# Counting one of six token tiles on ScalarE in a threshold search

## The chip, the cores and the metric

The kernel runs on one core of a Trainium2 chip. A core has a matrix engine (TensorE, PE in the profile), three engines for elementwise work (VectorE, DVE; ScalarE, ACT; GpSimd, POOL), an engine that here only issues transfers (SyncE, SP), and 16 DMA engines. Each engine has a queue of its own and works through it in the order in which the program put it there; engines wait for each other by semaphores. The metric is the time of one execution on the device in microseconds (us), the median of several runs.

## The reference

One layer of a streaming encoder for 1024 tokens of width 1024. After a modulated norm, one combined projection of 4816 columns gives the inputs of two attention branches and the merge gates. In the sparse branch each token picks the 256 keys with the highest index score, out of the keys of its own chunk of 64 and of all earlier chunks:

```
dots = jnp.einsum('bqhd,bkd->bqhk', qi[:, start:end], ki[:, :end])
score = jnp.einsum('bqh,bqhk->bqk', wi[:, start:end], jax.nn.relu(dots))
score = jnp.where(allowed[None], score, -jnp.inf)
_, idx = lax.top_k(score, kk)
```

Softmax and the weighted sum of the values then run over the picked keys. After both branches come the gated merge, the output projection, a second norm, and a mixture of 32 experts with two experts per token.

## The kernel before, in words

**Tokens.** The 1024 tokens are 8 tiles of 128. Tile i has (i+1)*128 keys. Tiles 0 and 1 need no search (at most 256 keys). Tiles 2 to 7 each have a table `score[i]` of 128 x (i+1)*128 floats in on-chip memory, and `masks[i]`, which holds a bf16 copy of the upper half of each score until the search ends and the finished mask from then on.

**The search.** `select(tiles)` finds each row's 256th highest score by setting the bits of a threshold one after the other, from bit 30 down to bit 0. For a bit, VectorE compares each tile of the group with its threshold and adds up the hits (L722, one pass over the tile; bits 30 to 16 read the bf16 copy, bits 15 to 0 the floats), then two operations on 128x3 numbers (L725, L727) settle the bit and set the next one. So one bit's passes must end before the next bit's begin. Two searches run interleaved, one for tiles 2, 3, 4 and one for tiles 5, 6, 7; the text calls one bit of both a round. After bit 0, seven operations per tile (L733 to L740) make the mask, with ties in order of index.

**What sets the order.** The program text is written by generators that a class `Feed` interleaves. The projection loops call `feed.unit(650)` after each unit, which is three 128x128 by 128x512 products (a three-term product of split floats, L166 to L168). Each unit gives the search a budget of 650 times `feed.share` ns, and the search puts operations into the queues until the sum of its own cost estimates has used it up: 0.52 ns per key and 70 per pass for bits above 15, 1.04 ns per key and 70 otherwise, 100 for each small operation. These estimates decide where in each queue a search operation stands, and nothing else.

**Stages around the search.** With u for the units counted from the first one of the index projection: columns FQ at u 112 to 175 (share 0.3), three chunks of gate columns at u 176 to 367 (share 1.05), FV at u 368 to 431, FK from u 432. Before FK the rest of the search is put into the queues (`feed.drain_search`). A gate chunk takes 64 units: 8 products of 128 tokens-by-columns tiles, in the groups of 16, 8, 8, 8, 8, 16 units (`gate_chunk`). Each product gathers in one of three PSUM buffers `mm`, taken in turn, and ScalarE empties it with a sigmoid (L826), then issues the store to `gate_d`. The 8 slices of the next chunk's weights are converted one by one: ScalarE makes `wh` (L160), GpSimd `wl` (L163). In FK, ScalarE copies and squares each product (L860, L756), VectorE sums and normalises it, and TensorE transposes the result (L641) in between its products.

Of the kernel before, what the change touches and what calls it, by code (L numbers as in the profile page):

```python
# [19 lines left out]
F32 = mybir.dt.float32  # L20
F32R = mybir.dt.float32r
BF = mybir.dt.bfloat16
# [3 lines left out]
AF = mybir.ActivationFunctionType  # L26
OP = mybir.AluOpType
# [3 lines left out]
P = 128  # L31
T = 1024
D = 1024
NT = T // P
# [36 lines left out]
def kernel(ctx, tc, x, c, positions, ada_w, ada_b, norm1_g, norm2_g, w_in, b_fgt, b_gate,  # L71
# [3 lines left out]
    V, A, G, PE = nc.vector, nc.scalar, nc.gpsimd, nc.tensor  # L75
# [12 lines left out]
    def dump(name, ap):  # L88
        if name in dbg:
            SY.dma_start(dbg[name], ap)  # L90
# [64 lines left out]
    def bc(ap, shape):  # L155
        return ap.to_broadcast(shape)
# [327 lines left out]
    masks = {b: kvp2.tile([P, (b + 1) * P], BF, name=f"mask{b}") for b in range(2, NT)}  # L484
# [33 lines left out]
    def wtile(name):  # L518
        bufs = 1 if name == "t1" else 2
        feed.take(name, bufs)  # L520
        return wk.tile([P, H, HD], F32, name=name, bufs=bufs)

    def rope(dst, src, n, i=None, eng=G):

        if i is None:
            c4 = bc(cos[:, :, None, :], [P, n, 2, 32])
            s3 = bc(sin, [P, n, 32])
        else:
            c4 = bc(cos[:, i, None, None, :], [P, n, 2, 32])
            s3 = bc(sin[:, i, None, :], [P, n, 32])  # L530
        s4 = src.rearrange("p n (a d) -> p n a d", a=2)
        d4 = dst.rearrange("p n (a d) -> p n a d", a=2)
        t4 = wtile("t1").rearrange("p n (a d) -> p n a d", a=2)
        eng.tensor_tensor(t4[:, :, 0], s4[:, :, 1], s3, op=OP.mult)
        eng.tensor_tensor(t4[:, :, 1], s4[:, :, 0], s3, op=OP.mult)
        V.tensor_tensor(d4, s4, c4, op=OP.mult)
        yield 2
        V.tensor_tensor(d4[:, :, 0], d4[:, :, 0], t4[:, :, 0], op=OP.subtract)
        V.tensor_tensor(d4[:, :, 1], d4[:, :, 1], t4[:, :, 1], op=OP.add)
        feed.give("t1")  # L540
# [83 lines left out]
    xs = sX.enter_context(tc.tile_pool(name="xs", bufs=1, side="right"))  # L624
    score = {b: xs.tile([P, (b + 1) * P], F32, name=f"score{b}") for b in range(2, NT)}
    jk = xs.tile([P, T], BF, name="jk")
# [3 lines left out]
    def turned_heads(src, stack, dst, eng=G):  # L630

        st = stack()
        A.activation(st[:, :, 0].bitcast(F32R), src, AF.Copy)
        yield 1
        eng.tensor_tensor(st[:, :, 1].bitcast(F32R), src, st[:, :, 0], op=OP.subtract)
        yield 6
        feed.give("qr")
        for g in range(2):
            tp = ptb.tile([P, 4, P], F32, name="tpB")
            for j in range(4):  # L640
                PE.transpose(tp[:, j, :], st[:, g * 4 + j], ident)  # L641
            if g == 1:
                feed.give("stack")
            yield 1
            A.activation(dst(g), tp, AF.Copy)

    KSEL, scored = 256, []

    def index_scores(i, ps):
        q = wtile("q")
        A.activation(q, ps, AF.Copy)  # L653
        yield 1
        qr = wtile("qr")
        yield from rope(qr, q, H, i)
        feed.give("q")
        yield 1
        feed.take("stack", 2)
        feed.take("qT", 2)  # L660
        qT = xsa.tile([P, H, P], F32, name="qT", bufs=2).bitcast(F32R)
        yield from turned_heads(qr, lambda: xsa.tile([P, H, 2, HD], F32, name="stackx", bufs=2),
                                lambda g: qT[:, g * 4:g * 4 + 4])
        yield 1
        n = (i + 1) * P
        last = None

        def weigh(h, c0, w, pd):
            rl = xs.tile([P, 512], F32, name="rl", bufs=3)
            A.activation(rl[:, :w], pd[:, :w], AF.Relu)  # L670
            sc = score[i][:, c0:c0 + w]
            wc = wix[:, i, h:h + 1]
            if h == 0:
                V.tensor_scalar(sc, rl[:, :w], wc, None, op0=OP.mult)
            else:
                V.scalar_tensor_tensor(sc, rl[:, :w], wc, sc, op0=OP.mult, op1=OP.add)

        for h in range(H):
            for c0 in range(0, n, 512):
                w = min(512, n - c0)  # L680
                pd = psx.tile([P, 512], F32, name="pd")
                PE.matmul(pd[:, :w], qT[:, h], ikh[:, c0:c0 + w], start=True, stop=False)
                PE.matmul(pd[:, :w], qT[:, h], ikl[:, c0:c0 + w], start=False, stop=True)
                if last:
                    weigh(*last)
                last = (h, c0, w, pd)
                yield 1 if c0 else 0
        weigh(*last)
        feed.give("qT")
        dump(f"score{i}", score[i])  # L690
        V.memset(score[i][0:CH, n - CH:n], LOW)

        yield 2
        A.activation(masks[i], score[i].bitcast(BF).rearrange("p (n two) -> p n two", two=2)[:, :, 1], AF.Copy)
        yield 1
        scored.append(i)
        for grp in ((2, 3, 4), (5, 6, 7)):
            if i in grp and set(grp) <= set(scored):
                feed.search.append(select(grp))

    def select(tiles):


        m = len(tiles)
        bits = xs.tile([P, m], U32, name="bits", bufs=2)
        drop = xs.tile([P, m], U32, name="drop", bufs=2)
        cnt = xs.tile([P, m], F32, name="cnt_", bufs=2)
        thr = bits.bitcast(F32)

        for g, i in enumerate(tiles):  # L710
            n = (i + 1) * P
            V.tensor_scalar(jk[:, :n], score[i], 0.0, 0.0, op0=OP.is_ge, op1=OP.add, accum_out=cnt[:, g:g + 1])
            yield n * 1.04 + 70
        V.tensor_scalar(drop, cnt, KSEL - 0.5, float(2 ** 31), op0=OP.is_lt, op1=OP.mult)
        V.tensor_scalar(bits.bitcast(I32), drop.bitcast(I32), 31, 1 << 30, op0=OP.arith_shift_right,
                        op1=OP.bitwise_xor)


        for b in range(30, -1, -1):
            for g, i in enumerate(tiles):  # L720
                n = (i + 1) * P
                V.tensor_scalar(jk[:, :n], masks[i] if b > 15 else score[i], thr[:, g:g + 1], 0.0, op0=OP.is_ge,  # L722
                                op1=OP.add, accum_out=cnt[:, g:g + 1])
                yield n * (0.52 if b > 15 else 1.04) + 70
            V.tensor_scalar(drop, cnt, KSEL - 0.5, float(2 ** b), op0=OP.is_lt, op1=OP.mult)  # L725
            yield 100
            V.scalar_tensor_tensor(bits, bits, (1 << b) >> 1, drop, op0=OP.bitwise_xor, op1=OP.bitwise_xor)  # L727
            yield 100
        for g, i in enumerate(tiles):
            n = (i + 1) * P  # L730
            s = score[i]
            th, need = thr[:, g:g + 1], cnt[:, g:g + 1]
            V.tensor_scalar(jk[:, :n], s, th, 0.0, op0=OP.is_gt, op1=OP.add, accum_out=need)  # L733
            V.tensor_scalar(need, need, -1.0, float(KSEL), op0=OP.mult, op1=OP.add)
            V.tensor_scalar(jk[:, :n], s, th, None, op0=OP.is_equal)
            cs = xs.tile([P, 512], F32, name="rl", bufs=3).bitcast(F16)
            V.tensor_tensor_scan(cs[:, :n], bc(ones[:, 0:1], [P, n]), jk[:, :n], 0.0, op0=OP.mult, op1=OP.add)
            V.scalar_tensor_tensor(jk[:, :n], cs[:, :n], need, jk[:, :n], op0=OP.is_le, op1=OP.mult)
            V.scalar_tensor_tensor(jk[:, :n], s, th, jk[:, :n], op0=OP.is_gt, op1=OP.add)
            V.tensor_scalar(masks[i], jk[:, :n], -1.0, -NEG, op0=OP.add, op1=OP.mult)  # L740
            yield n * 5.98 + 600
# [6 lines left out]

    feed.rate = 4
    tokens(C_IQ, spread(index_scores), (4, 7, 6, 5, 3, 2))  # L750
    feed.rate, feed.share = 2, 0.05

# [40 lines left out]
    for i in range(2):  # L793
        masks[i] = kvp3.tile([P, (i + 1) * P], BF, name=f"mask{i}")
        n = (i + 1) * P
# [560 lines left out]
    for s_ in range(NT + 1):  # L1356
# [6 lines left out]
        if s_ < NT:  # L1363
            g = dsa_scores(s_)
# [141 lines left out]
    key = rtp2.tile([P, P], F32, name="key")  # L1506
# [16 lines left out]
    cnt = rtp2.tile([P, NE], F32, name="cnt")  # L1523
# [652 lines left out]
```

## Time and profile before

| | us |
|---|---|
| median of 3 runs (1690.26 to 1699.87) | 1691.45 |
| the profiled execution | 1688.29 |
| its span (first to last instruction) | 1686.5 |
| PE busy | 1535.2 (91%) |
| VectorE busy | 1001.4 (59%) |
| ScalarE busy | 562.9 (33%) |
| GpSimd busy | 343.3 (20%) |

The page cuts the span into 40 slices of 42.2 us. A digit is the busy share of an engine in tenths; PEclk is the clock that TensorE was granted, in tenths of full speed. The search lies in slices 4 to 10 (about 195 to 455 us).

### The profile page before, as it was taken

What the parts mean: (1) busy time and instruction counts of PE and PEld (TensorE: products, weight loads), DVE (VectorE), ACT (ScalarE), POOL (GpSimd) and SP (SyncE); (2) the same over time, 40 slices, a digit from 0 to 9 for tenths busy, and PEclk for the clock granted to TensorE, in tenths of its full rate; (3) what the DMA queues carried; (4) which work ended last, traced back from release to release, by engine and by line L of the source; (5) the groups of instructions that cost most, each with busy time, mean ns of one, the idle gap of its engine ahead of it and who ended that gap; (6) DMA issues with size and microseconds to landing.
All of it is one profiled execution on the core that took longest, in us unless ns stands there. A gap on an engine that the chain in (4) does not pass through costs nothing. (4 is left out here: it accounts for less than half of the span.)

```text
span 1686.5 us, 29265 instructions
## 1 busy us (share of the span) xinstructions
PE 1535.2 (91%) x10694; PEld 1020.3 (60%) x10695; DVE 1001.4 (59%) x2562; ACT 562.9 (33%) x1278; POOL 343.3 (20%) x376
## 2 busy tenths in 40 slices
PE   5999999999299999999998999699999899989993
PEld 4877878888287677765555777444444444544441
DVE  6688889999941877667664866422433434244331
ACT  5576242222163776546543433111111111111110
POOL 3333422222041432211003400001111111111110
PEclk9999999999699999999999999899999999999997
DMA  9300333331003331454555764889999999999992
GB/s 295 117 26 26 106 106 92 98 100 51 0 13 123 84 83 26 132 195 149 160 163 159 198 230 176 332 316 340 380 372 354 372 364 366 354 360 362 364 343 74
DMA packets 162282, 335.65 MB, mean 199 GB/s; under 512 B 31927, under 2 KB 78039, under 8 KB 162128
## 3 DMA queue, kind: packets, MB, share of 16 engines
q1 hardware_dynamic: 136368, 295.25, 50.7%
q0 software_dynamic: 11776, 20.93, 5.8%
q10 hardware_dynamic: 13984, 17.50, 2.9%
q8 instruction: 87, 1.43, 0.4%
q14 instruction: 67, 0.55, 0.1%
HBM read 299.02 MB, written 36.75 MB: 199 GB/s over the span
## 5 line engine op out<-in xcount | busy, mean ns | idle before, releaser
L1934 PE MATMUL pab<-block,gx 128*32 128x256 f32 (+1 forms) x2752 | 242.1, 428 | 4.5 <-DMA block<-in_exp_w 3.3
L2000 DVE SCALAR_TENSOR_TENSOR ys<-py,inf,gt 32x256 f32<-32x256 f32 (+2 forms) x178 | 97.6, 548 | 136.3 <-PE py L1980 52.5
L1934 PEld LDWEIGHTS pab<-block,gx 128*32 128x32 f32 (+1 forms) x2752 | 105.5, 117 | 113.6 <-issue 53.4
L1914 ACT ACTIVATE gx<-tpe,aff 128x64 f32<-128x64 f32 (+2 forms) x124 | 42.4, 422 | 327.5 <-PE tpe L1905 327.5
L163 POOL TENSOR_TENSOR wl<-wraw,wh 128x512 fp32r<-128x512 f32 x68 | 91.3, 1353 | 192.6 <-ACT wh L160 189.4
L1800 DVE COPY inf<-tpe 128x2 f32<-128x2 f32 x32 | 5.1, 159 | 207.6 <-PE tpe L1780 207.6
L166 PE MATMUL mm<-wh,hh 128*128 128x512 f32 x304 | 122.6, 403 | 0.5 <-ACT q L653 0.4
L168 PE MATMUL mm<-wh,hl 128*128 128x512 f32 x304 | 119.5, 393 | 0.0
L167 PE MATMUL mm<-wl,hh 128*128 128x512 f32 x304 | 119.5, 393 | 0.0
L166 PE MATMUL mm<-hh,wh 128*128 128x512 f32 x256 | 100.5, 393 | 0.0
L168 PE MATMUL mm<-hh,wl 128*128 128x512 f32 x256 | 99.7, 389 | 0.0
L167 PE MATMUL mm<-hl,wh 128*128 128x512 f32 x256 | 99.6, 389 | 0.0
L1795 POOL DMA_INDIRECT hg<-h_d,ix x31 | 31.1, 1003 | 309.7 <-issue 224.0
L722 DVE TENSOR_SCALAR_CACHE_REDUCE jk<-score,bits 128x768 bf16<-128x768 f32 (+2 forms) x96 | 90.7, 944 | 1.7
L1987 POOL DMA_INDIRECT out<-ys,ix x32 | 47.1, 1472 | 214.5 <-DVE ys L2000 201.9
L1926 PE MATMUL pab<-block,gx 128*128 128x512 f32 x192 | 85.9, 600 | 0.5
L722 DVE TENSOR_SCALAR_CACHE_REDUCE jk<-mask,bits 128x768 bf16<-128x768 bf16 (+2 forms) x90 | 85.0, 944 | 1.6
L1960 ACT ACTIVATE tx<-tpe 128x256 f32<-128x256 f32 (+2 forms) x32 | 14.9, 464 | 160.2 <-PE tpe L1958 160.2
L1001 DVE CUSTOM_DVE_ANT_0 zt<-psf,fb 128x1024 f32<-128x1024 f32 (+7 forms) x64 | 48.1, 754 | 31.4 <-PE psf L1071 22.7
L168 PEld LDWEIGHTS mm<-wh,hl 128*128 128x128 f32 x304 | 57.7, 190 | 12.6
L166 PEld LDWEIGHTS mm<-wh,hh 128*128 128x128 f32 x304 | 57.8, 190 | 11.6 <-ACT q L653 0.8
L1980 PE MATMUL py<-block,tx 128*32 128x256 f32 x1152 | 64.8, 380 | 0.0
(447 smaller groups left out, 3413.9 us busy)
## 6 DMA issues: line engine op xcount, KB each, us to landing
block<-in_exp_w SPq DMA_DIRECT2D x384, 512.0 KB
wraw<-in_w_in SPq DMA_DIRECT2D x72, 256.0 KB
adw<-in_ada_w SPq DMA_DIRECT2D x16, 1024.0 KB
xt<-in_x SPq DMA_DIRECT2D x16, 512.0 KB
gt<-gate_d SPq DMA_DIRECT2D x32, 256.0 KB
gate_d<-q ACTq DMA_DIRECT2D x30, 256.0 KB
adaw<-in_ada_w SPq DMA_DIRECT2D x4, 1024.0 KB
xt<-in_ada_w SPq DMA_DIRECT2D x8, 512.0 KB
```

What stands on the lines that cost most here:

```text
L163: eb.tensor_tensor(lo, src, hi.bitcast(F32), op=OP.subtract)
L166: PE.matmul(ps, lh, rh, start=first, stop=False)
L167: PE.matmul(ps, lh, rl, start=False, stop=False)
L168: PE.matmul(ps, ll, rh, start=False, stop=last)
L722: V.tensor_scalar(jk[:, :n], masks[i] if b > 15 else score[i], thr[:, g:g + 1], 0.0, op0=OP.is_ge, op1=OP.add, accum_out=cnt[:, g:g + 1])
L1001: V.tensor_tensor_reduce(zt[:, :n], ps[:, :n], add, -0.125, -LOW, op0=OP.add, op1=OP.min, accum_out=st[:, 0:1])
L1914: A.activation(gx[:, k, :n], tp[:, k, :n], AF.Identity, scale=scale, bias=shift)
L1926: PE.matmul(ps[:, m * 512:(m + 1) * 512], gx[:, k], r[:, m, kk * 512:(kk + 1) * 512], start=k == 0, stop=last)
L1934: PE.matmul(ps[c * n:(c + 1) * n, g * 8 * n:(g + 1) * 8 * n].rearrange("p (m f) -> p m f", m=2), gx[:, k, g * n:(g + 1) * n], w[:, c], sta ...
L1980: PE.matmul(py[c * 32:(c + 1) * 32, g * 256:(g + 1) * 256], tx[:, g, q * 32:(q + 1) * 32], r[:, m, c * 256:(c + 1) * 256], start=q == 0 an ...
L1987: G.indirect_dma_start(out=out, out_offset=bass.IndirectOffsetOnAxis(ap=ix, axis=0), in_=ys, in_offset=None, compute_op=OP.add, bounds_che ...
L2000: V.scalar_tensor_tensor(ys[r, f], py[c * n:(c + 1) * n, g * w:(g + 1) * w], inf[r, 6:7], gt2[r, f], op0=OP.mult, op1=OP.mult)
```

## The change

Tile 7, the longest, is counted on ScalarE. For it the search puts into ScalarE's queue one pass `Sign(threshold - score)` over 128x1024 with a running sum (new L728) and one 128x1 operation that turns the sum into the count that the settling step expects (new L730); VectorE's pass for that tile goes. The ScalarE pass adds 0 to the cost estimate (`yield 0`). It always reads the floats, so the bf16 copy of tile 7 (L694) is no longer made; its elementwise output goes to `masks[7]` as a place to write. Tile 7 comes first in its group. Since a sum of signs treats a score equal to the threshold otherwise than a comparison does, tile 7 gets six more VectorE operations after bit 0 (one pass over 1024 keys, five on 128x1).

```diff
-    KSEL, scored = 256, []
+    KSEL, ON_A, scored = 256, NT - 1, []
...
-        A.activation(masks[i], score[i].bitcast(BF).rearrange("p (n two) -> p n two", two=2)[:, :, 1], AF.Copy)
+        if i != ON_A:
+            A.activation(masks[i], score[i].bitcast(BF).rearrange("p (n two) -> p n two", two=2)[:, :, 1], AF.Copy)
...
+        tiles = sorted(tiles, key=lambda i: i != ON_A)
...
+        sums = xs.tile([P, 2], F32, name="sums", bufs=2) if ON_A in tiles else None
...
         for b in range(30, -1, -1):
             for g, i in enumerate(tiles):
                 n = (i + 1) * P
+                if i == ON_A:
+                    A.activation(masks[i], score[i], AF.Sign, scale=-1.0, bias=thr[:, g:g + 1],
+                                 accum_out=sums[:, 0:1])
+                    A.activation(cnt[:, g:g + 1], sums[:, 0:1], AF.Copy, scale=-0.5, bias=0.5 * n + 0.25)
+                    yield 0
+                    continue
                 V.tensor_scalar(jk[:, :n], masks[i] if b > 15 else score[i], thr[:, g:g + 1], 0.0, op0=OP.is_ge,
                                 op1=OP.add, accum_out=cnt[:, g:g + 1])
...
+            if i == ON_A:
+                ulp = sums[:, 1:2]
+                V.scalar_tensor_tensor(ulp, th, -1.0, th, op0=OP.mult, op1=OP.max)
+                V.scalar_tensor_tensor(th, ulp, 2.0 ** -126, th, op0=OP.is_ge, op1=OP.mult)
+                V.tensor_scalar(jk[:, :n], s, th, 0.0, op0=OP.is_gt, op1=OP.add, accum_out=need)
+                V.tensor_scalar(ulp, ulp, 1.2 * 2.0 ** -24, None, op0=OP.mult)
+                V.scalar_tensor_tensor(ulp, need, KSEL - 0.5, ulp, op0=OP.is_ge, op1=OP.mult)
+                V.tensor_tensor(th, th, ulp, op=OP.add)
```

**VectorE, one late round.** Before (`score5` to `score7` are tiles 5 to 7, `cnt__1662` the counts of that group, `jk` a scratch output):

```order
L722 TENSOR_SCALAR jk_856,cnt__1662<-score5_853,bits_1660 128x768
L727 SCALAR_TENSOR_TENSOR bits_2108<-bits_2108,drop_2109 128x3
L722 TENSOR_SCALAR jk_856,cnt__1662<-score6_854,bits_1660 128x896
L722 TENSOR_SCALAR jk_856,cnt__2110<-score2_850,bits_2108 128x384
L722 TENSOR_SCALAR jk_856,cnt__1662<-score7_855,bits_1660 128x1024
L722 TENSOR_SCALAR jk_856,cnt__2110<-score3_851,bits_2108 128x512
L725 TENSOR_SCALAR drop_1661<-cnt__1662 128x3
L722 TENSOR_SCALAR jk_856,cnt__2110<-score4_852,bits_2108 128x640
```

Now:

```order
L733 TENSOR_SCALAR jk_856,cnt__1661<-score5_853,bits_1659 128x768
L733 TENSOR_SCALAR jk_856,cnt__2113<-score2_850,bits_2111 128x384
L733 TENSOR_SCALAR jk_856,cnt__1661<-score6_854,bits_1659 128x896
L733 TENSOR_SCALAR jk_856,cnt__2113<-score3_851,bits_2111 128x512
L736 TENSOR_SCALAR drop_1660<-cnt__1661 128x3
L733 TENSOR_SCALAR jk_856,cnt__2113<-score4_852,bits_2111 128x640
L738 SCALAR_TENSOR_TENSOR bits_1659<-bits_1659,drop_1660 128x3
```

The 1024-wide pass is gone; four passes stand between the setting of the bits and the step L736 that needs ScalarE's count.

**ScalarE, the end of the second gate chunk and the start of the third.** Before (`wh` is a converted weight slice, `mm` a PSUM buffer, `q` the sigmoid's output):

```order
L160 ACTIVATE wh_3285<-wraw_2977 128x512
L160 ACTIVATE wh_3298<-wraw_3224 128x512
L826 ACTIVATE q_3308<-mm_3201,bgc_70 128x512
L827 DMA gate_d_79<-q_3308 128x512
L826 ACTIVATE q_3311<-mm_3202,bgc_70 128x512
L827 DMA gate_d_79<-q_3311 128x512
L160 ACTIVATE wh_3321<-wraw_3238 128x512
L160 ACTIVATE wh_3337<-wraw_3253 128x512
L826 ACTIVATE q_3399<-mm_3314,bgc_70 128x512
```

Now:

```order
L728 ACTIVATE mask7_801,sums_1662<-score7_855,bits_1659 128x1024
L730 ACTIVATE cnt__1661<-sums_1662 128x1
L160 ACTIVATE wh_3364<-wraw_3026 128x512
L160 ACTIVATE wh_3378<-wraw_3297 128x512
L846 ACTIVATE q_3388<-mm_3275,bgc_70 128x512
L847 DMA gate_d_79<-q_3388 128x512
L846 ACTIVATE q_3391<-mm_3276,bgc_70 128x512
L847 DMA gate_d_79<-q_3391 128x512
L160 ACTIVATE wh_3401<-wraw_3315 128x512
L728 ACTIVATE mask7_801,sums_1662<-score7_855,bits_1659 128x1024
L730 ACTIVATE cnt__1661<-sums_1662 128x1
L160 ACTIVATE wh_3419<-wraw_3329 128x512
```

The last two of the 31 passes L728 (bits 1 and 0) stand ahead of, and between, the sigmoids and conversions of the second chunk's end. All 31 stand in ScalarE's queue ahead of the third chunk's first sigmoid: 4 in FQ, 27 from the first gate unit on. The last search operation of VectorE stood in the middle of FV before and now stands in the third gate chunk. No table load of ScalarE is added, and no transfer of SP's queue changes place.

## Rows read from the trace of the kernel before

**Rows 1.** The page, part 2: busy tenths and granted clock in 40 slices.
```profile
PE   5999999999299999999998999699999899989993
DVE  6688889999941877667664866422433434244331
PEclk9999999999699999999999999899999999999997
```
**Rows 2.** Stretches: us, PE, PEld, DVE, ACT, POOL busy (x), PEclk, DMA share, GB/s.
```profile
238.70:412.80 174.10, 174.10 (x769) 144.01 (x769) 168.29 (x435) 45.59 (x72) 41.82 (x36) 1.00 0.29 88
432.60:462.30 29.70, 0.01 (x2) 0.04 (x1) 26.79 (x48) 3.55 (x9) 1.88 (x2) 0.56 0.00 0
462.30:495.00 32.70, 32.70 (x157) 27.13 (x158) 15.43 (x34) 17.28 (x39) 10.34 (x9) 0.93 0.04 11
```
**Rows 3.** Waits, longest first: us in total, times, longest.
```profile
PE tpB L641 <- DVE stack L635: 29.7, 1, 29.7
```
**Rows 4.** Timeline of DVE: start, duration; the first gate-phase round to the mask's end.
```profile
244.55 1.14 DVE L722 TENSOR_SCALAR_CACHE_REDUCE jk<-mask,bits 128x896 bf16<-128x896 bf16 x1
246.39 1.28 DVE L722 TENSOR_SCALAR_CACHE_REDUCE jk<-mask,bits 128x1024 bf16<-128x1024 bf16 x1
...
398.04 1.28 DVE L722 TENSOR_SCALAR_CACHE_REDUCE jk<-score,bits 128x1024 bf16<-128x1024 f32 x1
...
399.37 0.75 DVE L722 TENSOR_SCALAR_CACHE_REDUCE jk<-score,bits 128x512 bf16<-128x512 f32 x1
...
404.06 1.28 DVE L722 TENSOR_SCALAR_CACHE_REDUCE jk<-score,bits 128x1024 bf16<-128x1024 f32 x1
...
416.76 1.28 DVE L722 TENSOR_SCALAR_CACHE_REDUCE jk<-score,bits 128x1024 bf16<-128x1024 f32 x1
...
419.88 1.01 DVE L733 TENSOR_SCALAR_CACHE_REDUCE jk<-score,bits 128x768 bf16<-128x768 f32 x1
...
454.69 0.33 DVE L740 TENSOR_SCALAR mask<-jk 128x640 bf16<-128x640 bf16 x1
```
**Rows 5.** Timeline of ACT: end of FQ, end of FV, and the queue around the 30 us.
```profile
238.72 0.60 ACT L777 ACTIVATE q<-mm 128x512 f32<-128x512 f32 x1 [1.41 <-PE mm L168]
...
412.92 1.28 ACT L844 ACTIVATE vf<-mm 128x512 f32<-128x512 f32 x2 [1.36 <-PE mm L168]
...
424.77 0.61 ACT L860 ACTIVATE q<-mm 128x512 f32<-128x512 f32 x1
455.65 0.60 ACT L756 ACTIVATE sq<-mm 128x512 f32<-128x512 f32 x1 [30.27 <-DVE sm L758]
```
**Rows 6.** Groups by line, ACT: count | busy us, mean ns | idle before.
```profile
L160 ACT ACTIVATE wh<-wraw 128x512 fp32r<-128x512 f32 x72 | 44.3, 631 | 28.7 <-PE mm L167 12.4 <-PE mm L168 10.6 <-DMA wraw<-in_w_in 3.9
L826 ACT ACTIVATE q<-mm,bgc 128x512 f32<-128x512 f32 x30 | 20.7, 689 | 94.9 <-PE mm L168 89.0 <-ACT q L826 2.8 <-DMA gate_d<-q 2.6
L1004 ACT ACTIVATION_READ_ACCUMULATOR zt<-zt,smf 128x1 f32 x64 | 12.4, 194 | 0.0
L401 ACT ACTIVATE hh<-xT,mod 128x1024 fp32r<-128x1024 f32 x8 | 9.5, 1235 | 3.6 <-DVE mod L397 3.6
L1004 ACT ACTIVATE zt<-zt,smf 128x1024 f32<-128x1024 f32 x8 | 9.1, 1143 | 0.2
L294 ACT ACTIVATE jx<-xt 128x1024 bf16<-128x1024 f32 x8 | 8.4, 1050 | 2.4 <-DMA xt<-in_x 2.4
L172 ACT ACTIVATE smo<-smo 128x1 f32<-128x1 f32 x8 | 1.6, 196 | 1.9 <-DVE smo L171 1.9
```
**Rows 7.** Short stretches around the wait, columns as in group 2.
```profile
432.00:437.00 5.00, 0.60 (x3) 0.18 (x1) 4.75 (x10) 0.00 (x0) 0.00 (x0) 0.94 0.00 0
437.00:442.00 5.00, 0.00 (x0) 0.00 (x0) 4.86 (x7) 0.00 (x0) 0.00 (x0) 0.50 0.00 0
466.00:467.00 1.00, 1.00 (x3) 0.73 (x3) 0.00 (x0) 0.15 (x1) 0.00 (x0) 0.50 0.00 0
467.00:468.00 1.00, 1.00 (x6) 0.80 (x5) 0.00 (x0) 0.00 (x0) 0.00 (x0) 0.95 0.00 0
```

## The prediction

> **What bounds the kernel now.** I read the page's slices first, to find the stage that the search touches. TensorE is at nine tenths nearly throughout, except one slice at 2, the eleventh (422 to 464 us), and there its granted clock is the lowest, too. VectorE is at nine tenths in the five slices up to it [rows 1]. So the search sets the time in one place. The list of waits names it: one wait of 29.7 us, TensorE for `stack`, which VectorE writes in FK [rows 3]. The table of stretches shows the same from both sides: from 238.7 to 412.8 TensorE never pauses (769 products, 256 units, 0.680 us each) while VectorE is 97% busy; from 432.6 to 462.3 TensorE does nothing [rows 2]. The timeline of VectorE tells what it does meanwhile: bit 0's last passes, and from 419.9 to 455.0 the masks [rows 4]; only then come FK's sums.
>
> Two readings matter more than that wait. **The queue lags behind its text.** A clear round takes 404.06 - 398.04 = 6.02 us [rows 4], but the planner books a round above bit 15 at 3.0 us (4224 keys x 0.52, six passes x 70, four small steps x 100) and a lower one at 5.2. So VectorE's search operations stand in the text well ahead of when VectorE gets to them. Before, that hurts nobody, since TensorE and ScalarE wait for no search result until FK. **What a waiting ScalarE holds up.** ScalarE's square for FK waited 30.27 us for VectorE, with all of FK's later evictions behind it [rows 5].
>
> **The change, part by part.**
>
> *Removed from VectorE:* 31 passes of 1024 keys. One takes the slot 398.04 to 399.37, 1.33 us [rows 4], so a clear round falls from 6.02 to 4.69. It is no cheaper on the bf16 copy: the pass at 246.39 also took 1.28 [rows 4].
>
> *Added to ScalarE:* 31 times Sign with a sum. The trace has no Sign, so I bound it by 1024-wide rows: 1.05 us (a square to bf16) and 1.24 (identity to split floats); nearest is Exp with a sum, 1.14, and its accumulator read 0.19; the 128x1 step after it 0.20 [rows 6]. With gaps 1.6 us. VectorE asks for the count after four passes (of 768, 384, 896, 512 keys, some 3.6 us of the 4.69), so ScalarE has 2 us to spare at either bound and the round stays 4.69. In sum 50 us on an engine that is busy for 45.6 of the 174.1 us [rows 2]: room enough. The bf16 copy that goes and the operations after bit 0 that come (one pass, 1.3 us, and five tiny ones, together about 2) cost nothing: the masks now end near 412 and FK starts some 45 us later; without that cover it would be 2 us.
>
> *Moved, and here is the cost:* each Sign waits for a bit that VectorE has to set, and behind it in ScalarE's queue stand sigmoids that free PSUM buffers, and conversions of the next weights. With three buffers TensorE can run one or two products ahead of a sigmoid, no more. So the lag of VectorE, until now free, becomes TensorE's pace. Even the cheaper rounds are slower than booked (2.4 us above bit 15, 4.1 below), so VectorE stays behind to the end.
>
> **The sum.** First VectorE. The order has four rounds ahead of the gates, where the trace had three; so 27 rounds are left, and I let them start where the first gate-phase round did, at 244.6 [rows 4]. Before, 27 rounds took 416.76 - 246.39 = 170.4 us, 8 more than 27 x 6.02; in that time GpSimd converted four chunks' slices, and I charge the 8 us to its work. Two chunks' conversions fall into the new rounds: 4 us. Rounds end at 244.6 + 27 x 4.69 + 4 = 375.2, bit 1's Sign starts two rounds earlier, at 365.8.
>
> Then TensorE. The third chunk's first pair of products needs two buffers. The second of them is freed by a sigmoid that stands behind bit 1's Sign and two conversions: 365.8 + 1.6 + 2 x 0.63 + 0.69 [rows 6] = 369.4. From there 127 units lie ahead of FK, without any Sign in the way that matters: 127 x 0.680 = 86.4, FK starts at 455.8. Is TensorE really waiting then? Its last long stop before is for a sigmoid behind bit 11's Sign: 244.6 + 15 x 4.69 + 2 + 1.6 + 0.69 = 319.2; from there 63 units take it to 362. So it waits some 7 us again. Without any stop TensorE would have been at this unit at 238.7 + 129 x 0.680 = 326.4, so the stops add up to 43 us; by the places of the sigmoids there are five, of 5 to 11 us each.
>
> The clock: after the end of products at 432.6 the granted clock averaged 0.94 up to 437 and was 0.50 after, and after the restart at 462.3 it stayed at 0.50 (1.2 GHz) until about 467 [rows 7]: 4.7 us at half speed, 2.4 us lost. In the long wait it was down in the second 5 us, so I take it to be down after a stop of 7 us as well and charge 2.4 us for the last one. For the earlier ones I charge nothing, because TensorE waits for ScalarE again after each.
>
> Before, FK started at 412.8 and then lost 29.7 and 2.4 us, as if it had started at 444.9. Now: 455.8 + 2.4 = 458.2, with no wait in FK. So **+13.3 us**. Behind FK every stage waits for the one ahead (the expert weights, too, are loaded into space that the attention gives back), so I carry it to the end in full: 1688.3 (the profiled execution) + 13 = **1701 us**. The median of the runs stands 3 us above that execution; against it the same sum would be 1704.
>
> Bounds of the unknown parts: with no loss to GpSimd and no slow clock 1688.3 + 6.9 = 1695; with all 8 us for GpSimd and a Sign that takes 1.24 + 0.4, 1705.
>
> **The rivals.**
>
> *The load simply moves.* VectorE's end comes 31 x 1.33 = 41 us earlier, which is more than the wait of 29.7, so the wait and its slow restart vanish: 1688.3 - 32 = 1656. For it: ScalarE's free time, and VectorE being full in these slices. Against it: the order, in which all 31 Signs stand ahead of the third chunk's first sigmoid, and three buffers. It decides if the planner's text and VectorE run at the same pace, which rounds of 6.02 us against 3.0 booked exclude. Chance 0.07. The Trainium skill, Perfetto Trace Analysis, section Optimizing Scalar/DVE Operations, says that with VectorE saturated it may make sense to hand some work to ScalarE. By that rule the time would be this rival's; the trace agrees only that VectorE is saturated, not that its end is all that counts.
>
> *Stops at the lower clock feed back.* If the clock falls at each of the five stops, and a product at 1.2 GHz (twice as long) is then late for the sigmoid ahead of the next Sign, VectorE waits for ScalarE, and the stops are no longer swallowed: 5 x 2.4 = 12 us instead of 2.4, 1711. For it: the clock's fall in the long wait [rows 7], and the pair of sigmoids just ahead of bit 8's Sign, which TensorE reaches within 2 us of VectorE by my sum. Against it: elsewhere in the queue the sigmoids have several us to spare. It decides from about 2 us of lateness on. Chance 0.20. The Trainium skill, TensorE: Matmul & The Clock Gate, section HAM oscillation, describes kernels in which recurring waits let the clock fall again and again and every burst starts slow. By it this rival would be the time; the one long wait here agrees, the short ones no row here shows.
>
> *Drag and gain cancel.* If ScalarE gets its sigmoids out earlier than I think, for instance because the first rounds start earlier than 244.6, the drag is about the size of the tail that goes: 1688 to 1692. Against it: the floor above, 1695, has only VectorE's own passes in it. Chance 0.13.
>
> **How the numbers follow.** Forecast 0.60, the rivals 0.07, 0.20, 0.13. The range reaches from the cancelling case, 1690, to a little above the feedback case, 1714; outside are the simple move and the ends of the others. A measurement of this kernel can tell about 1%, 17 us, from no change: faster by more than that is the first rival alone, 0.07; slower by more (above 1708) is the feedback case and the forecast's upper edge, 0.24; within 1%, 0.69.
>
> **What would show it.** In the profile after: VectorE's late rounds at 4.7 us, none longer except during conversions; VectorE's masks done near 412, then long idle; no wait of TensorE for `stack` in FK, but several of 5 to 11 us between 255 and 370 us, released by the sigmoid or by the conversions; ScalarE idle ahead of Sign for VectorE; FK's first copy near 469; a lower clock in slices 6 to 8. I would be wrong if TensorE ran through the gate chunks without a stop (then the first rival), or if VectorE's rounds were longer than 5 us throughout because ScalarE's counts come late (then the second).

## The result, and the profile after

The changed kernel takes **1714.45 us** (median of 4 runs, 1711.8 to 1718.45) against 1690.93 for the kernel before in the same comparison; the ratio is 1.0131, 95% interval 1.01 to 1.0162. It is slower by 1.3%. The forecast had the sign and the mechanism and was 10 us short: in the profiled executions, 1711.8 against 1688.29, the loss is 23.5 us where 13.3 were forecast. The median lies at the upper edge of the range, 0.45 us above its 1714, and among the results that the prediction set apart it is "slower by more" than 1%, which had a chance of 0.24 against 0.69 for "within 1%".

The slices of the page after, now of 42.8 us, to be read against [rows 1]: TensorE's gap in the eleventh slice is gone, and smaller ones stand in the seventh and eighth, with a lower clock in both.

```profile
PE   5999985689999999899999899789999899989993
DVE  6688779999043677676763866432343434244331
PEclk8999997799999999999999999899999999999996
```

The lists of waits (us in total, times, longest) answer to [rows 3]. TensorE has no wait for `stack` left. It waits for the sigmoids instead, ScalarE waits ahead of Sign for VectorE's bits, and VectorE, done early, waits 49.5 us for FK's first square.

```profile
PE mm L166 <- ACT q L846: 40.3, 5, 11.0
...
ACT mask L728 <- DVE bits L738: 66.6, 25, 4.4
...
DVE sm L778 <- ACT sq L776: 54.4, 4, 49.5
```

TensorE's timeline (start, duration, last bracket: idle before and its releaser) shows the five stops, each ended by a sigmoid:

```profile
270.00 0.80 PE L166 MATMUL mm<-hh,wh 128*128 128x512 f32 x1 [11.02 <-ACT q L846]
...
294.45 0.80 PE L166 MATMUL mm<-hh,wh 128*128 128x512 f32 x1 [6.00 <-ACT q L846]
...
304.23 0.80 PE L166 MATMUL mm<-hh,wh 128*128 128x512 f32 x1 [8.13 <-ACT q L846]
...
325.81 0.80 PE L166 MATMUL mm<-hh,wh 128*128 128x512 f32 x1 [8.61 <-ACT q L846]
...
379.12 0.79 PE L166 MATMUL mm<-hh,wh 128*128 128x512 f32 x1 [6.58 <-ACT q L846]
```

ScalarE's timeline shows why, at the last stop, and where FK begins. Behind the Sign of bit 1 (375.97) stand its accumulator read, the count, two conversions and the first sigmoid (378.40 to 379.07); TensorE restarts at 379.12. FV's last copy starts at 467.04, so FK starts at 466.9 (412.8 in [rows 5]); FK's first copy is at 477.92.

```profile
375.97 1.15 ACT L728 ACTIVATE mask<-score,bits 128x1024 bf16<-128x1024 f32 x1 [2.87 <-DVE drop L736]
377.03 0.19 ACT L728 ACTIVATION_READ_ACCUMULATOR mask<-score,bits 128x1 f32 x1
377.25 0.20 ACT L730 ACTIVATE cnt__1661<-sums 128x1 f32<-128x1 f32 x1
377.36 1.13 ACT L160 ACTIVATE wh<-wraw 128x512 fp32r<-128x512 f32 x2
378.40 0.67 ACT L846 ACTIVATE q<-mm,bgc 128x512 f32<-128x512 f32 x1
...
467.04 1.28 ACT L864 ACTIVATE vf<-mm 128x512 f32<-128x512 f32 x2 [1.36 <-PE mm L168]
...
477.92 0.60 ACT L880 ACTIVATE q<-mm 128x512 f32<-128x512 f32 x1 [8.56 <-PE mm L168]
```

The stretches (columns as in group 2 of the rows before) give the whole, some ten microseconds about three stops, and the way from the last stop to FK. In the stretch of [rows 2] that held 769 products without a pause, TensorE now does 532.

```profile
238.70:412.80 174.10, 131.81 (x532) 105.33 (x531) 163.58 (x429) 66.32 (x129) 26.16 (x25) 0.87 0.22 68
...
260.00:270.00 10.00, 0.00 (x1) 0.00 (x1) 9.72 (x29) 3.46 (x7) 0.00 (x0) 0.69 0.00 0
290.00:300.00 10.00, 1.65 (x3) 0.83 (x3) 9.72 (x29) 3.46 (x7) 0.00 (x0) 0.55 0.07 27
300.00:310.00 10.00, 5.77 (x17) 4.65 (x18) 9.72 (x30) 4.04 (x8) 0.00 (x0) 0.60 0.09 32
...
379.12:466.90 87.78, 87.78 (x379) 72.48 (x380) 48.87 (x77) 22.43 (x35) 24.20 (x18) 0.98 0.26 79
```

Last, VectorE's timeline, against [rows 4]: what holds the first round of the gate stage up (244.76), one clear round (258.26 to 263.15), and one beside GpSimd's conversions.

```profile
244.76 0.20 DVE L171 TENSOR_SCALAR q<-rdq 128x64 f32<-128x64 f32 x1 [2.94 <-DMA fq_d<-q]
...
248.02 1.00 DVE L733 TENSOR_SCALAR_CACHE_REDUCE jk<-mask,bits 128x768 bf16<-128x768 bf16 x1
...
257.98 0.17 DVE L736 TENSOR_SCALAR drop<-cnt__2113 128x3 uint32<-128x3 f32 x1
258.19 0.16 DVE L738 SCALAR_TENSOR_TENSOR bits<-bits,drop 128x3 uint32<-128x3 uint32 x1
258.26 1.01 DVE L733 TENSOR_SCALAR_CACHE_REDUCE jk<-mask,bits 128x768 bf16<-128x768 bf16 x1
...
263.15 1.01 DVE L733 TENSOR_SCALAR_CACHE_REDUCE jk<-mask,bits 128x768 bf16<-128x768 bf16 x1
...
323.80 1.01 DVE L733 TENSOR_SCALAR_CACHE_REDUCE jk<-score,bits 128x768 bf16<-128x768 f32 x1
...
328.30 1.08 DVE L738 SCALAR_TENSOR_TENSOR bits<-bits,drop 128x3 uint32<-128x3 uint32 x1
329.30 0.16 DVE L736 TENSOR_SCALAR drop<-cnt__2113 128x3 uint32<-128x3 f32 x1
329.49 1.12 DVE L738 SCALAR_TENSOR_TENSOR bits<-bits,drop 128x3 uint32<-128x3 uint32 x1
330.54 1.00 DVE L733 TENSOR_SCALAR_CACHE_REDUCE jk<-score,bits 128x768 bf16<-128x768 f32 x1
```

A clear round, one without GpSimd's conversions, is 263.15 - 258.26 = 4.89 us, not 4.69: the two small steps for tiles 2, 3, 4 (L736, L738), the second of which reads the first's result, now stand back to back and start 0.21 us apart. The round from 323.80 took 6.74 us: both L738 steps took about 1.1 us instead of 0.16. In the same 2.5 us GpSimd converted two slices (timeline of GpSimd):

```profile
328.07 2.53 POOL L163 TENSOR_TENSOR wl<-wraw,wh 128x512 fp32r<-128x512 f32 x2 [4.47 <-ACT wh L160]
```

### The profile page after: what moved, and what is told of

It reads as the page before. It is cut to its first block, busy times and chain, and to the rows that moved or that the text cites. A ratio compares the mean times of both kernels' runs of the same rounds, so it can differ in the third digit from the quotient of the medians.

```text
span 1710.0 us, 29314 instructions
## 1 busy us (share of the span) xinstructions
PE 1543.7 (90%) x10694; PEld 1022.7 (60%) x10695; DVE 974.0 (57%) x2507; ACT 603.4 (35%) x1370; POOL 344.0 (20%) x376
## 5 line engine op out<-in xcount | busy, mean ns | idle before, releaser
L166 PE MATMUL mm<-hh,wh 128*128 128x512 f32 x256 | 105.1, 411 | 41.4 <-ACT q L846 40.3
L168 PE MATMUL mm<-hh,wl 128*128 128x512 f32 x256 | 103.2, 403 | 0.9 <-POOL wl L163 0.9
L167 PE MATMUL mm<-hl,wh 128*128 128x512 f32 x256 | 103.3, 404 | 0.0
L166 PEld LDWEIGHTS mm<-hh,wh 128*128 128x128 f32 x256 | 50.4, 197 | 54.7 <-ACT q L846 42.8
L733 DVE TENSOR_SCALAR_CACHE_REDUCE jk<-score,bits 128x768 bf16<-128x768 f32 (+4 forms) x80 | 70.2, 877 | 1.7
L733 DVE TENSOR_SCALAR_CACHE_REDUCE jk<-mask,bits 128x768 bf16<-128x768 bf16 (+4 forms) x75 | 65.7, 876 | 1.4
L728 ACT ACTIVATE mask<-score,bits 128x1024 bf16<-128x1024 f32 x31 | 35.6, 1149 | 84.3 <-DVE bits L738 66.6
```

What stands on the lines that cost most here:

```text
L166: PE.matmul(ps, lh, rh, start=first, stop=False)
L167: PE.matmul(ps, lh, rl, start=False, stop=False)
L168: PE.matmul(ps, ll, rh, start=False, stop=last)
```

## The experiments

Theory A is the prediction's: the waiting Signs in ScalarE's queue tie TensorE, through the sigmoids behind them, to VectorE's rounds. Theory B is that the added ScalarE work itself is what costs.

**1. The same ScalarE work without the wait, and none of it.** In both kernels tile 7's count is a constant, set ahead of the loop by lines that are not shown.

```diff
# free_sign
-  A.activation(masks[i], score[i], AF.Sign, scale=-1.0, bias=thr[:, g:g + 1], accum_out=sums[:, 0:1])
-  A.activation(cnt[:, g:g + 1], sums[:, 0:1], AF.Copy, scale=-0.5, bias=0.5 * n + 0.25)
+  A.activation(masks[i], score[i], AF.Sign, scale=-1.0, bias=ones[:, 0:1], accum_out=sums[:, 0:1])
+  A.activation(sums[:, 1:2], sums[:, 0:1], AF.Copy, scale=-0.5, bias=0.5 * n + 0.25)
# no_sign: both lines away
```

> ScalarE does the same 31 Sign passes and 31 small steps at the same places of its queue, but Sign compares with a constant and the sum goes to a scratch column, so neither engine waits for the other; tile 7's search result is left out (its threshold is fixed). Theory A (the stops come from ScalarE waiting for VectorE's bits, with sigmoids and conversions queued behind): the five stops go, FK starts near 414 us, the masks end near 425, total 1656 to 1664. Rival B (ScalarE's 50 us of extra work delays the sigmoids): total stays above 1700.

> As free_sign, but without ScalarE's passes: the price of VectorE's relief alone; tile 7's count is left out. Theory A: within 3 us of free_sign, 1655 to 1663. Rival B: at least 30 us below free_sign.

Measured: free_sign **1660.83 us** (1658.43 to 1661.95), ratio 0.9821 (0.9798 to 0.9844); no_sign 1666.35 in a single run. In both, TensorE is busy through all 174.1 us of the stretch; here free_sign's, with 83 us of ScalarE work in it:

```profile
238.70:412.80 174.10, 174.10 (x770) 144.11 (x769) 167.96 (x426) 83.05 (x153) 44.28 (x33) 1.00 0.28 85
```

So the 31 Signs by themselves cost nothing that shows: no_sign is no faster, and that it was 5.5 us slower, outside its expectation, is one run and has no cause shown. B falls. The wait alone is worth 1714.45 - 1660.83 = 54 us.

**2. The planner's estimates set to what the passes take,** in the changed kernel and, as a control, in the one before. The rows of the search then stand later in the text, nearer to when VectorE gets to them.

```diff
-  yield n * (0.52 if b > 15 else 1.04) + 70     # each pass; also the pass ahead of bit 30
+  yield n * 1.04 + 265
...
-  yield n * 5.98 + 600                          # the mask of a tile
+  yield n * 5.98 + 1500
```

> Only the planner's cost estimates of the changed kernel are corrected to the measured slots (1.04 ns per key plus 265 ns for every pass, 1500 instead of 600 ns for a mask). Theory A: Sign then stands in the queue where VectorE has nearly arrived, the five stops shrink to a sum under 12 us; fewer rounds fit ahead of the gates, so VectorE ends near 432 and FK waits about 10 us: 1662 to 1676. Rival B: the work is the same, total stays above 1700.

> The same corrected estimates in the kernel before. Theory A: no engine of the gate stage waits for the search there, so the text's lead was free; the total does not fall. One or two rounds move from FQ, where VectorE has gaps, into the gates: 1690 to 1702. If the estimates were worth something by themselves, it would fall below 1685.

Measured: est_after 1674.12 us (1668.9 to 1679.02), ratio 0.989 (0.9864 to 0.9917); est_before 1701.55, ratio 1.0065 (1.0043 to 1.0087). The same edit takes 40 us off the changed kernel and adds 11 to the one before. In est_after, TensorE's waits are

```profile
PE mm L166 <- ACT q L846: 6.5, 2, 5.6
PE tpB L641 <- DVE stack L635: 5.9, 1, 5.9
```

In est_before TensorE waits for no sigmoid, and the later search only makes FK's wait longer, 41.4 us for 29.7 in [rows 3]:

```profile
PE tpB L641 <- DVE stack L635: 41.4, 1, 41.4
```

**3. Six PSUM buffers for the gate products instead of three,** alternating between two pools.

```diff
-  pss = {t2: pm.tile([P, 512], F32, name="mm") for t2 in grp}
+  pss = {}
+  for t2 in grp:
+      turn[0] ^= 1
+      pss[t2] = psx.tile([P, 512], F32, name="pd") if turn[0] else pm.tile([P, 512], F32, name="mm")
```

> The changed kernel, with six PSUM buffers for the gate products in place of three. Theory A (TensorE stops because the sigmoids that free its three buffers stand behind waiting Signs): with three buffers more it runs ahead of the sigmoids by another half chunk, the stops after 250 us become shorter in sum (under 36 us against 40.3), the median comes down a little, 1700 to 1711, because in the end TensorE is still tied to VectorE's rounds and to the weight conversions, which stand behind the same Signs. Rival (the buffers don't bind; what binds is only ScalarE's queue, in which the weight conversions of the next chunk stand too): the stops move from the q buffers to the weights and the time stays at 1712 to 1717.

Measured: 1710.42 us (1706.39 to 1713.15), ratio 1.0101 (1.007 to 1.0133), an interval that overlaps that of the change. Its time and the sum of its five stops, 33.7 us, are in A's ranges; what the stops wait for is what the rival named. No stop is for a sigmoid, all five are for converted weight slices, and one of them lasts 26.55 us:

```profile
313.92 0.79 PE L166 MATMUL pd<-hh,wh 128*128 128x512 f32 x1 [26.55 <-ACT wh L160]
```

So both things that the prediction named behind the Signs bind, the sigmoids first and the weights next, and more buffers alone buy nothing that can be told from no change.

**4. Tile 7 last in its group,** so that a pass stands between the two small steps again (ph2).

```diff
-  tiles = sorted(tiles, key=lambda i: i != ON_A)
+  tiles = sorted(tiles, key=lambda i: i == ON_A)
```

> The changed kernel, with tile 7 last in its group instead of first, so that the two small operations on the bits of one group have a pass of the other group between them again. Theory A (the round's extra 0.20 us is the two small dependent operations standing back to back): the 128x768 passes come every 4.69 us in clear rounds instead of 4.89, 25 rounds end 5 us earlier, TensorE's stops on q are 2 to 5 us shorter in sum, median 1706 to 1711: still slower than before. Rival (the extra 0.20 us is the wait for ScalarE's count, or the passes themselves): the round stays at 4.89 or grows, median 1713 to 1718.

Measured: **1703.29 us** (1697.93 to 1709.64, 10 runs), ratio 1.0064 (1.0041 to 1.0086): 11 us off, where 4 to 8 were expected. VectorE's timeline: between the two steps for tiles 2, 3, 4 (256.22, 257.24) now lies the 768-key pass, and a round is 260.99 - 256.30 = 4.69 us.

```profile
242.19 1.00 DVE L733 TENSOR_SCALAR_CACHE_REDUCE jk<-mask,bits 128x768 bf16<-128x768 bf16 x1
...
256.22 0.17 DVE L736 TENSOR_SCALAR drop<-cnt__2110 128x3 uint32<-128x3 f32 x1
256.30 1.01 DVE L733 TENSOR_SCALAR_CACHE_REDUCE jk<-mask,bits 128x768 bf16<-128x768 bf16 x1
257.24 0.08 DVE L733 DVE_READ_ACCUMULATOR jk<-mask,bits 128x1 f32 x1
257.24 0.16 DVE L738 SCALAR_TENSOR_TENSOR bits<-bits,drop 128x3 uint32<-128x3 uint32 x1
...
260.99 1.01 DVE L733 TENSOR_SCALAR_CACHE_REDUCE jk<-mask,bits 128x768 bf16<-128x768 bf16 x1
```

Not expected: the first round of the gate stage also starts 5.8 us earlier, at 242.19 instead of 248.02. One half of it is the wait for the `fq_d` transfer, 0.15 us here instead of 2.94 (more on it below). The other half is there before: FQ's last products come 2.8 us earlier (ScalarE's copies of them start at 236.20 instead of 239.03). In the change a Sign beside FQ, at 220.62, held ScalarE for 2.02 us, and TensorE then stopped for 1.76 us, up to 226.35; ph2 has neither. FK's first copy comes at 465.19 (477.92 after the change, near 469 by the prediction).

**5. The parts together.** est_after_fq is est_after with `feed.share` 0.55 instead of 0.3 beside FQ; est_ph is est_after with the order of ph2; est_ph_fq has all three.

```diff
-  feed.share = 0.3        # beside FQ
+  feed.share = 0.55
```

> The changed kernel with the planner's estimates set to the measured pass times (as in est_after, 1674.1) and a larger share of that work beside the FQ projection (0.55 for 0.3), so that more Signs stand ahead of the gate stage. Theory A (what est_after still loses is the last drag of TensorE by the rounds, 6.5 us of stops on q, and the 5.9 us wait for VectorE's stack): the rounds start earlier by up to one or two of them (4.9 to 9.8 us), both waits shrink, 1662 to 1672. Rival (FQ's own evictions now stand behind Signs, or the rounds lose to FQ's VectorE work what they gain): 1672 to 1680, with new stops of TensorE before 240 us.

> All three together: measured estimates, the larger share beside FQ, and tile 7 last in its group. Theory A: the clear round is 4.69 us, so some 5 us come off VectorE's chain beside what the larger share gives: 1656 to 1668, ahead of est_after (1674.1) and close to the kernel whose Signs wait for nothing (free_sign, 1660.8). Rival (VectorE's chain no longer decides, or the other order makes Sign the round's last step): equal to est_after_fq within 2 us.

> Measured estimates and tile 7 last in its group, without the larger share beside FQ. Theory 1 (the larger share gives nothing by itself, as est_after_fq against est_after says; the gain of est_ph_fq is the shorter round): 1659 to 1665, equal to est_ph_fq (1661.6). Theory 2 (the earlier start of the rounds and the shorter round are both needed, because each alone only moves the wait from TensorE's q buffers to VectorE's stack): 1666 to 1672, between est_after (1674.1) and est_ph_fq, with a stop on q or a wait for stack of 4 us or more.

| | median us | ratio to before (95%) | TensorE waits: `q`, `stack` |
|---|---|---|---|
| est_after | 1674.12 | 0.989 (0.9864 to 0.9917) | 6.5, 5.9 |
| est_after_fq | 1675.07 | 0.9881 (0.9831 to 0.993) | 7.8, none |
| est_ph | 1674.61 | 0.9897 (0.9853 to 0.9941) | 2.4, 10.6 |
| est_ph_fq | **1661.62** | 0.9812 (0.9764 to 0.9859) | 2.0, none |

est_after_fq missed A's range and fell into its rival's. The wait for `stack` is gone, but the waits for sigmoids are a little longer, and the rival's sign, new stops ahead of 240 us, is there: from 200 to 240 us TensorE is busy for 36.81 us, in est_after for all 40.00. The longest of the three stops is for VectorE:

```profile
227.14 1.03 PE L614 MATMUL tpB<-ident,fl 128*8 128x128 f32 x8 [1.77 <-DVE fl L607]
```

est_ph has the long wait for `stack` that its second theory named, but its median is 2.6 us above that theory's range: the shorter round alone brought no time that its runs, spread over 11 us, could show. Together they did: est_ph_fq is as fast as the kernel whose Signs wait for nothing (1660.83), beats the kernel before by 1.9% and, by the medians of separate comparisons, the change by 3%, and its gate stage is nearly without stops:

```profile
238.70:412.80 174.10, 171.99 (x757) 141.45 (x756) 168.84 (x439) 79.61 (x150) 41.14 (x31) 1.00 0.27 82
```

Why either part alone gains nothing and both gain 12 us is told here by the waits only; a run that separates the last microseconds was not made.

## Why the prediction was right, and where it was short

**The drag: right, and shown.** Five stops, 40.3 us in sum (43 by the prediction), all behind Signs; no wait for `stack`; VectorE idle for 49.5 us after its masks. Experiment 1 shows that the wait does it and not the load, experiment 2 that it goes as the Signs move back in the queue, experiment 3 that both the sigmoids and the weights behind the Signs carry it.

**Sign's own price: right.** 1149 ns, and 186 and 203 for what follows, against 1.14, 0.19 and 0.20 taken from Exp, its accumulator read and the 128x1 step [rows 6]:

```profile
L728 ACT ACTIVATE mask<-score,bits 128x1024 bf16<-128x1024 f32 x31 | 35.6, 1149 | 84.3 <-DVE bits L738 66.6 <-DVE drop L736 8.7 <-DVE bits L719 8.6
...
L730 ACT ACTIVATE cnt__1661<-sums 128x1 f32<-128x1 f32 x31 | 6.3, 203 | 1.0
L728 ACT ACTIVATION_READ_ACCUMULATOR mask<-score,bits 128x1 f32 x31 | 5.8, 186 | 0.0
```

VectorE never waited for a count in the gate stage, as forecast.

**From the last stop to FK: right, the clock a little too dear.** Forecast 3.55 us from bit 1's Sign to TensorE's restart and 88.8 from there to FK, the clock's 2.4 in it; measured 379.12 - 375.97 = 3.15 and 87.8. That is 1.4 us less than forecast, 1.0 of it in the clock's term: 87.8 is 1.4 above 127 x 0.680.

**When bit 1's Sign starts: short by 10.1 us,** 375.97 where the sum had 244.6 + 25 x 4.69 + 4 = 365.85. Three terms of the step "First VectorE" were mis-sized:

- *The start of the rounds, +3.4.* It was taken from the trace of before, 244.6; it is 248.02. A Sign beside FQ started only at 233.12, 2.29 us after ScalarE was free for it; four weight conversions stood behind it, and SyncE's queue, which loads the next weights into the space that the conversions free, reached the last stores of `fq_d` late (timeline of SyncE's queue):

```profile
231.26 9.35 SPq L442 DMA_DIRECT2D wraw<-in_w_in  x6
240.70 0.86 SPq L800 DMA_DIRECT2D fq_d<-q  x2
```

  Before, the same six loads were issued within 6.73 us and the stores at 239.35. VectorE's next step then waited 2.94 us for that transfer. So the drag had begun one stage ahead of the gates, by way of a third queue, to which the prediction did not follow it. The late issue is only part of it: the stores were issued 1.35 us later than before, the step that waits for them ran 3.2 us later (244.76; 241.57 before, without a wait), and what made the transfer itself take longer was not tested. In ph2 the stores are issued at 236.82, the wait is 0.15 us, and the rounds start at 242.19:

```profile
228.43 7.26 SPq L442 DMA_DIRECT2D wraw<-in_w_in  x6
236.82 1.30 SPq L800 DMA_DIRECT2D fq_d<-q  x2
```

- *The clear round, +5.0.* 4.89 instead of 4.69 over 25 rounds. The prediction took the 1024-key pass's slot off a round and did not look at what the new order set next to each other. The order printed ahead of the prediction ends before those rows. ph2 undoes it and measures 4.69.
- *GpSimd, +1.7.* Charged 4 us; the rounds up to bit 1 are 5.7 us longer than 25 clear ones (375.97 - 248.02 - 25 x 4.89).

3.4 + 5.0 + 1.7 = 10.1, less the 1.4, is the 8.7 us by which FK starts late: 466.9 against 458.2. The rest of the 23.5, that is 23.5 - (466.9 - 444.9) = 1.5 us, lies behind FK: the first load of `fq_d` after FK is still 22.1 us later than before (531.2, 509.1). Its cause is open.

**The masks near 412: wrong, at no cost.** They ended at 429.5: the rounds ended late, and the last two tiles' masks fell beside GpSimd's conversions. FK's first square was 49 us away.

**The rivals.** *The load simply moves*, 1656, is what free_sign measures without the wait, 1660.83. The Trainium skill, Perfetto Trace Analysis, section Optimizing Scalar/DVE Operations, says that it may make sense to hand work to ScalarE when VectorE is saturated; the runs agree where the handed work waits for nothing (1660.83) or hardly (1661.62), and not for the change as it was made, 54 us above the first.

*Stops at the lower clock feed back*, 1711, gives the measured time, and half of it is true: the clock did fall at each of the five stops, to 0.50 (1.2 GHz; the 0.55 to 0.69 above are means over both levels), and the 532 products of the stretch took 131.81 us where 532 x 0.2264 = 120.4 would have done at the pace of [rows 2], 11.4 us lost. But the other half fails, narrowly, at the very place that the prediction had named. Ahead of bit 8's Sign ScalarE waited 1.82 us for TensorE's product, and the Sign started at 340.81, 0.65 us later behind its bits than the others:

```profile
338.57 0.69 ACT L846 ACTIVATE q<-mm,bgc 128x512 f32<-128x512 f32 x1 [1.82 <-PE mm L168]
...
340.81 1.15 ACT L728 ACTIVATE mask<-score,bits 128x1024 bf16<-128x1024 f32 x1 [0.40 <-ACT q L846]
```

Its count was there at 342.29, and VectorE asked for it at 343.88; that round, from 340.32 to 345.21, took 4.89 us like the clear ones. The rounds that were longer, 5.35 to 6.74 us, lie beside GpSimd's conversions. So the slow clock never reached VectorE, and the next stop took the loss in. The agreement with 1711 is an accident: the three terms above make up the difference, and ph2, with five stops as well (33.6 us), comes to 1703.29 with the round alone and its start mended. The Trainium skill, TensorE: Matmul & The Clock Gate, section HAM oscillation, describes waits that let the clock fall again and again; the trace agrees with the fall at each stop, but here what was lost behind the first four stops only shortened the next wait, and behind the last one it was 1.4 us.

*Drag and gain cancel* needed an earlier start of the rounds; it was later.

## What to carry to other kernels

Work that is handed to an idle engine brings its wait along: before moving it, list what stands behind the waiting instruction in that engine's queue, and who is fed by it. If the text is ordered by estimated costs, an engine that falls behind its estimates costs nothing until something waits for it, and then its whole lag becomes the pace of the others; so correct the estimates together with the move (here that took 40 us off, and with two smaller edits 1.3% slower became 1.9% faster). When a step leaves a round-robin, read the new neighbours of the steps that stay: 0.20 us between two dependent small steps came to 5 us.

## What the runs showed of the hardware

- A 128x3 step of VectorE that takes 0.16 us took 0.5 to 1.3 us in the changed kernel while GpSimd converted 128x512 slices (1.08 and 1.12 us at 328.30 and 329.49), while the comparing passes kept their 0.6 to 1.15 us. Each of the 15 stretched steps (L736 and L738) between 228 and 390 us ends within 0.06 us of the end of a conversion, as at 330.61 and 330.60 above (the ends inside a row of several conversions are an estimate, the row divided evenly). The 14 of ph2 and the 21 of the kernel before do so, too, with the conversions at other times. No run took GpSimd away. The Trainium skill, SBUF — State Buffer, section Who interferes with whom, says that a VectorE instruction with two inputs in on-chip memory contends with a GpSimd instruction that reads it, and that a `tensor_scalar` can contend, too, under conditions that no run here tests, but not the form that also writes out its accumulator. The trace agrees: L738, with two such inputs, and L736, a plain `tensor_scalar` (0.82 us at 368.35, 1.29 at 381.40), are stretched, and the compares with their sum (1.00 us at 330.54, 1.01 at 258.26) are not.
- The granted clock fell in stops far shorter than the one of before. In the stop of 11.02 us it was 0.50, the lower of its two levels (1.2 GHz), from 264 to 270 us, and 1.00 again from 274 to 288 us, with TensorE busy; from 300 to 304 us, in the stop of 8.13 us, it was 0.50, too.
- Two dependent 128x3 steps back to back started 0.21 us apart (257.98, 258.19); a pass that followed such a step without needing its result started 0.08 us after it (256.22, 256.30 in ph2).
